# A trunk layer on one core: small products held behind the last large product traced ahead of them, with one or two more generator steps between some operands and their products

## The chip, the cores and the metric

The kernel runs on one core of one Trainium2 chip. The metric is device microseconds for one execution of the whole layer. Engines are named as in the profile: PE (TensorE matmul), DVE (VectorE), ACT (ScalarE), POOL (GpSimd), and SP, whose queue issues the DMAs.

## The reference

One layer of a conditioned decoder trunk, sequence 1024, width 1024. What matters here is the token mixer: one input projection feeds four branches of width 256, of which these are touched by the change:

```
def gla_chunked(q, k, v, log_a):            # 4 heads of 64
    def step(state, chunk):
        b = jnp.cumsum(lac, axis=2)
        q_dec = qc * jnp.exp(b)
        attn = jnp.where(causal, jnp.einsum('bhtd,bhsd->bhts', q_dec, kc * jnp.exp(-b)), 0.0)
        o = jnp.einsum('bhtd,bhde->bhte', q_dec, state) + jnp.einsum('bhts,bhse->bhte', attn, vc)
        k_dec = kc * jnp.exp(bL - b)
        state = jnp.exp(bL[:, :, 0, :])[..., None] * state + jnp.einsum('bhsd,bhse->bhde', k_dec, vc)
...
    a, g = jnp.split(p["conf"], 2, axis=-1)
    u = causal_dwconv(a * jax.nn.sigmoid(g), conf_dw_w) + conf_dw_b      # 31 taps
    u = jax.nn.silu(layer_norm(u, conf_ln_g, conf_ln_b))
...
    gates = jax.nn.sigmoid(p["gate"] + merge_gate_b).reshape(Bn, S, N_BRANCH, D_MODEL)
    merged = (gates[:, :, 0] * y_ml + ... + gates[:, :, 3] * y_sc)
    return merged @ w_o
```

An mLSTM branch of the same form as the gated linear attention (GLA) stands beside it. The layer ends with an output projection and a feed-forward part.

## The kernel before, in words

The weights are multiplied in a Strassen-like scheme: a pair of projections is made of seven large products (11, T2, 21, T1, T3, T4, 22), each of twelve 128x512 matmuls. The time runs through stages: the first norms and modulations; P, twelve such pairs (`pair`, called here P00 to P11); G, eight first halves of the gates (`gate_first`, numbered 0 to 7); then the rest of the gates with the merge (E), the output projection and the feed-forward part.

In P and G the branches' own small work runs between the large products. It is written as Python generators (`ml_all`, `gla_all`, `conf_mix` and what they call). After each large product `pull(rate, crate)` advances them by some steps, one step to the next `yield`. The scheduler then orders each engine by its own estimated timeline, so that a small product can move ahead of or behind the place where it was traced. POOL is kept in program order in P and G. The profile records every instruction at one line (159, a helper), so the source lines below are those of the program.

The pieces that the prediction speaks of:

- `tok_v` (line 891) turns the values of a branch from channel-major to token-major: eight transposes for each half of the channels, from a tile `p` that a DMA fills (`p<-dgv`). `tok_load` (line 904) issues both loads, but the second goes into the buffer that the first leaves free.
- `conf_mix` (line 805): 4 x 30 taps of the convolution on DVE (line 817) and a bias on ACT (820); sums over channels by a matrix of ones on PE (825), one group for each half of the sequence; DVE subtracts the mean (827); ACT squares (830, 831); sixteen one-column matmuls sum the squares (836).
- `gla_mix` (line 1116), eight chunks. For each chunk: scores, eight groups of small products `kx` by `qb` (1162), with operands from ACT exponentials and DVE multiplications in `prep` (1145, 1146); DVE masks the scores into `at` (1168); transposes of the decayed keys (1186), copied by ACT to `kw` (1188); the output from the state and from `at` (1191, 1194); then `kw` by `v`, which updates the state (1198).
- `gate_first` (line 634): first product (643), an ACT copy of its result (646), second product into the same accumulator (648), an ACT copy (651), a DMA to `dz` (652). The second product must wait for the first copy.

```
        prod(ps, wnext.pop(0), "11", True)
...
        A.copy(t[:, 0, :], ps)
        yield
        prod(ps, wnext.pop(0), "21", False)
...
        A.copy(t[:, 1, :], ps)
        nc.sync.dma_start(dz[4 * n + p], t)
```

- `lm[0]` holds the last large matmul that was traced; `prod` sets it.

Of the kernel before, what the change touches and what calls it, by code (L numbers as in the profile page):

```python
# [16 lines left out]
P = 128  # L17
# [129 lines left out]
def trunk_layer(ctx: ExitStack, tc: tile.TileContext, I, out, dump=None, stop=None):  # L147
# [14 lines left out]

    V, A, G, T = (InOrder(e, n) for e, n in ((nc.vector, "V"), (nc.scalar, "A"), (nc.gpsimd, "G"), (nc.tensor, "T")))
# [641 lines left out]
    def conf_mix():  # L805
# [16 lines left out]
        for h in range(2):  # L822
            ps = mps()
            for j in range(2):
                T.matmul(ps, ones, y[:, j, HH[h]], start=(j == 0), stop=(j == 1))
            for j in range(2):
                V.scalar_tensor_tensor(y[:, j, HH[h]], ps, -1.0 / MIX, y[:, j, HH[h]], ALU.mult, ALU.add)
            yield
# [5 lines left out]
        for a in range(NCH):  # L834
            for i, s_ in enumerate((s0, s1_)):
                T.matmul(ps[:, a:a + 1], s_[:, a * P:(a + 1) * P], one, start=(i == 0), stop=(i == 1))
# [3 lines left out]
        for h in range(2):  # L840
            ps = mps()
            rows_bc(r[:, 4 * h:4 * h + 4], 4, ps)
# [48 lines left out]
    def tok_v(v, j, vc):  # L891
        for h in range(2):
            ps = mps()
            for c in range(4):
                T.transpose(ps[:, c * P:(c + 1) * P], vc[:, (4 * h + c) * P:(4 * h + c + 1) * P], ident)
# [8 lines left out]
    def tok_load(nm):  # L904
# [5 lines left out]
        yield  # L910
        for j in range(2):
# [4 lines left out]
    def ml_all():  # L916
        vt = new_v("V")
        yield
# [13 lines left out]
    def ml_rows():  # L932
# [45 lines left out]
        for n, r in enumerate((a, w1, w0)):  # L978
            T.transpose(ps[:, 32 * n:32 * n + 32], r, ident[0:32, 0:32])
# [5 lines left out]
    def ml_mix(dnm, dwi, cols, v):  # L985
# [31 lines left out]
        for c in range(NCH):  # L1017
            e, q, kt, wi, qb = nxt_
            ps = mps()
            for j in range(2):  # L1020
                T.matmul(ps[:, j * MIX:(j + 1) * MIX], kt[:, j, :], qb[:, j].rearrange("p x t -> p (x t)"),
# [5 lines left out]
            for j in range(2):  # L1027
                T.transpose(pk[:, j * P:(j + 1) * P], kt[:, j, :], ident)
# [5 lines left out]
            for j in range(2):  # L1034
                w = 2 * (DH + 1)
                T.matmul(po[:, j * w:(j + 1) * w], qw[:, j, :], cn[:, j, :, :], start=True, stop=False)
                for x in range(2):
                    h = 2 * j + x
                    o = h * (DH + 1)
                    T.matmul(po[:, o:o + DH + 1], e[:, h, :], v[:, c, h, :], start=False, stop=(x == 1))  # L1040
# [7 lines left out]
            for j in range(2):  # L1048
                T.matmul(pc_[:, j * w:(j + 1) * w], kw[:, 2 * j:2 * j + 2, :], v[:, c, 2 * j:2 * j + 2, :],
# [17 lines left out]
    def head_norm(v, mul, dst):  # L1067
# [9 lines left out]
        for h in range(2):  # L1077
# [3 lines left out]
            for c in range(4):  # L1081
# [3 lines left out]
                for j in range(2):  # L1085
                    T.transpose(ps[j][:, c * P:(c + 1) * P], hf[:, j * P:(j + 1) * P], ident)
# [6 lines left out]
    def gla_decay():  # L1093
# [3 lines left out]
        for j in range(2):  # L1097
            t0, t1 = c4(), c4()
            for h in range(2):
                ps = mps()  # L1100
                T.matmul(ps, a2[64:96, j * P:(j + 1) * P], m2[64:96, HH[h]], start=True, stop=True)
# [14 lines left out]
    def gla_mix(v):  # L1116
# [37 lines left out]
        yield  # L1154
        for c in range(NCH):
# [3 lines left out]
            for j in range(2):  # L1159
                for i in range(NSB):  # L1160
                    m = (i + 1) * SB
                    T.matmul(ps4[0:m, j, :, i, :], kx[:, j, i, 0:m], qb[:, j, :, i * SB:m], start=True, stop=True)
# [15 lines left out]
            yield  # L1178
            if c + 1 < NCH:
                nxt_ = prep(c + 1, *raw1)  # L1180
            if c + 2 < NCH:
# [754 lines left out]
```

## Time and profile before

| | |
|---|---|
| median of 3 runs | 1636.38 us (1635.22 to 1641.09) |
| profiled execution | 1636.97 us, span 1635.2 us, so 1.8 us lie outside the span |
| PE busy | 1541.4 us, 94% of the span |
| DVE, ACT, POOL busy | 72%, 57%, 45% |
| mean granted TensorE clock | 0.97 |

Times in the views count from the start of the span. An operation's name is its output, an arrow, its inputs, by the program's names: `b` is a PSUM accumulator, `wh` and `wl` the two parts of a split weight, `cst` the identity, `cn` a branch's state.

### The profile page before, as it was taken

To read this page: it belongs to the slowest core of one execution; us is meant where nothing else is said; L and a number is where in the kernel's file an instruction comes from. 1 tells how busy PE (TensorE), PEld (TensorE's weight loads), DVE (VectorE), ACT (ScalarE), POOL (GpSimd) and SP (SyncE) were. 2 spreads that over 40 slices of the span, in tenths; PEclk is the share of its full clock that TensorE was granted. 3 is DMA by queue.
4 is the path that set the end of the run, shared out by engine and by line. 5 is a ranking of instruction groups with operands and counts; after the bars stand their busy time and mean duration, and the time that the engine had idled before them with its cause. 6 is when DMAs were issued, how large, how long until landed. Compare 5 with 4: busy or idle time off the path is not lost.

```text
span 1635.2 us, 21394 instructions
## 1 busy us (share of the span) xinstructions
PE 1541.4 (94%) x6885; PEld 1247.2 (76%) x6885; DVE 1179.4 (72%) x1955; ACT 928.8 (57%) x1718; POOL 732.5 (45%) x617
## 2 busy tenths in 40 slices
PE   7799799998998999999999999999999998999996
PEld 5677588876876777878788877778888887777885
DVE  7876886989555657766783769398888666555678
ACT  7465444344675453535454757566556655678973
POOL 1455365543343335747630224444445431866115
PEclk8799999999999999999999999999999999999997
DMA  9244325433357545454523564644444317455243
GB/s 363 69 148 130 100 88 148 130 110 106 104 191 242 159 142 164 127 184 129 173 78 97 193 213 149 208 152 162 140 155 142 99 65 256 158 167 178 66 129 122
DMA packets 133268, 242.70 MB, mean 148 GB/s; under 512 B 14052, under 2 KB 33092, under 8 KB 133156
## 3 DMA queue, kind: packets, MB, share of 16 engines
q1 hardware_dynamic: 132660, 241.10, 45.5%
q8 instruction: 54, 0.88, 0.2%
q14 instruction: 58, 0.48, 0.1%
q10 hardware_dynamic: 496, 0.23, 0.1%
HBM read 191.70 MB, written 49.58 MB: 148 GB/s over the span
## 4 chain that ended last, share of the span: by engine, by line
PE 70%; DVE 8%; DMA 8%; ACT 4%; issue 4%; POOL 2%; SPq 0%; DVEq 0%; POOLq 0%; ACTq 0%
PE b L159 70%; DVE c L159 2%; DVE wl L159 1%; DMA T<-dg 1%; DVE T L159 1%; DVE acc L159 1%; ACT b L159 1%; DMA s2d<-in_ada_b_dram 1%; ACT wh L159 1%; DMA wr<-in_wu_dram 1%; ACT B L159 1%; DVE B L159 1%; DMA c<-in_wt_dram 1%; DVE b L159 1%; DVE mg L159 1%
## 5 line engine op out<-in xcount | busy, mean ns | idle before, releaser
L159 PE MATMUL b<-B,wh 128*128 128x512 f32 (+1 forms) x1704 | 542.5, 401 | 30.5 <-DVE B L159 17.7
L159 PE MATMUL b<-T,wh 128*128 128x512 f32 x1512 | 482.9, 399 | 6.2 <-ACT wh L159 2.5
L159 PEld LDWEIGHTS b<-B,wh 128*128 128x128 f32 x1704 | 326.4, 195 | 103.7 <-DVE B L159 20.7
L159 PE MATMUL b<-B,wl 128*128 128x512 f32 (+1 forms) x840 | 335.2, 400 | 21.2 <-DVE wl L159 18.5
L159 PEld LDWEIGHTS b<-T,wh 128*128 128x128 f32 x1512 | 285.6, 190 | 73.2 <-ACT wh L159 3.4
L159 PE MATMUL b<-T,wl 128*128 128x512 f32 x752 | 298.0, 398 | 4.2 <-DVE wl L159 3.5
L159 PEld LDWEIGHTS b<-B,wl 128*128 128x128 f32 x840 | 162.9, 194 | 61.7 <-DVE wl L159 24.2
L159 PEld LDWEIGHTS b<-T,wl 128*128 128x128 f32 x752 | 142.7, 190 | 38.2 <-DVE wl L159 4.6
L159 ACT CAST wh<-wr 128x512 fp32r<-128x512 f32 x159 | 97.2, 616 | 112.0 <-PE b L159 81.6
L159 PE MATMUL b<-T,fh 128*128 128x512 f32 x368 | 116.2, 397 | 0.8 <-ACT fh L159 0.8
L159 DVE SCALAR_TENSOR_TENSOR b<-c,par,b 128x512 f32<-128x512 f32 x132 | 97.0, 751 | 25.9 <-ACT b L159 25.8
L159 DVE TENSOR_TENSOR c<-b,c 128x512 f32<-128x512 f32 x132 | 90.1, 685 | 19.5 <-PE b L159 15.2
L159 POOL TENSOR_TENSOR mg<-mg,c 128x512 f32<-128x512 f32 x48 | 63.0, 1332 | 75.6 <-DVE c L159 75.0
L159 ACT ACTIVATE c<-c,hpar 128x1024 f32<-128x1024 f32 (+1 forms) x34 | 37.5, 1104 | 102.2 <-DVE c L159 99.6
L159 DVE SCALAR_TENSOR_TENSOR b<-G,par,b 128x512 f32<-128x512 f32 x120 | 89.8, 748 | 1.3
L159 ACT ACTIVATE b<-c,par 128x512 f32<-128x512 f32 x88 | 57.4, 683 | 53.5 <-DVE c L159 53.1
L159 PEld LDWEIGHTS b<-T,fh 128*128 128x128 f32 x368 | 69.2, 188 | 17.9 <-ACT fh L159 1.2
L159 ACT CAST b<-wr 128x512 fp32r<-128x512 f32 x105 | 61.2, 586 | 35.3 <-DVE c L159 12.3
L159 PE MATMUL b<-B,wbh 128*128 128x512 f32 x256 | 80.4, 397 | 0.0
L159 DVE TENSOR_TENSOR wl<-wr,b 128x512 fp32r<-128x512 f32 x82 | 55.6, 681 | 25.0 <-ACT b L159 16.8
L159 PE MATMUL b<-T,fl 128*128 128x512 f32 x184 | 72.2, 395 | 0.0
L159 POOL TENSOR_TENSOR B<-B,B 128x512 f32<-128x512 f32 x29 | 43.3, 1492 | 59.7 <-DVE wl L159 56.6
(394 smaller groups left out, 2916.7 us busy)
## 6 DMA issues: line engine op xcount, KB each, us to landing
wr<-in_wu_dram SPq DMA_DIRECT2D x70, 256.0 KB, 2.7
B<-in_wg_dram SPq DMA_DIRECT2D x61, 256.0 KB, 3.5
fr<-in_wu_dram SPq DMA_DIRECT2D x50, 256.0 KB, 3.0
dg<-c SPq DMA_DIRECT2D x22, 512.0 KB, 2.9
T<-in_ada_a_dram SPq DMA_DIRECT2D x16, 512.0 KB, 9.5
wr<-in_wo_dram SPq DMA_DIRECT2D x32, 256.0 KB, 2.6
wr<-in_wp_dram SPq DMA_DIRECT2D x30, 256.0 KB, 2.8
wx<-in_wp_dram SPq DMA_DIRECT2D x24, 256.0 KB, 2.7
```

What stands on the lines that cost most here:

```text
L159: ins = f(*a, **k)
```

## The change

A class `Behind` wraps the tensor engine: each small product issued through `B` is placed after `lm[0]`, the last large matmul traced before it; the scheduler may not put it earlier on PE. It is used for the sums of `conf_mix`, the transposes of `tok_v`, the rows and chunks of the mLSTM, the head norms, and the decay and chunks of the GLA. Besides, `tok_load` gets two more `yield`s between the loads and the first transposes, `ml_all` two more, `gla_mix` one more ahead of its loop, and within a chunk `prep` of the next chunk moves ahead of a `yield`. The number of instructions stays the same on every engine; only their order changes, on PE from the place that ran at about 231 us to the one at 542 us.

```
+    class Behind:
+        def __getattr__(self, op):
+            def call(*a, **k):
+                with tc.issue_after(lm[0]):
+                    return getattr(T, op)(*a, **k)
+            return call
+
+    B = Behind()
...
             for j in range(2):
-                T.matmul(ps, ones, y[:, j, HH[h]], start=(j == 0), stop=(j == 1))
+                B.matmul(ps, ones, y[:, j, HH[h]], start=(j == 0), stop=(j == 1))
...
-                T.matmul(ps[:, a:a + 1], s_[:, a * P:(a + 1) * P], one, start=(i == 0), stop=(i == 1))
+                B.matmul(ps[:, a:a + 1], s_[:, a * P:(a + 1) * P], one, start=(i == 0), stop=(i == 1))
...
-            rows_bc(r[:, 4 * h:4 * h + 4], 4, ps)
+            with tc.issue_after(lm[0]):
+                rows_bc(r[:, 4 * h:4 * h + 4], 4, ps)
...
-                T.transpose(ps[:, c * P:(c + 1) * P], vc[:, (4 * h + c) * P:(4 * h + c + 1) * P], ident)
+                B.transpose(ps[:, c * P:(c + 1) * P], vc[:, (4 * h + c) * P:(4 * h + c + 1) * P], ident)
...
             nc.sync.dma_start(vcs[j], dp[nm][:, j, :])
         yield
         yield
+        yield
+        yield
         for j in range(2):
             tok_v(vt, j, vcs[j])
...
         vt = new_v("V")
+        yield
+        yield
         yield
...
-                    T.transpose(ps[j][:, c * P:(c + 1) * P], hf[:, j * P:(j + 1) * P], ident)
+                    B.transpose(ps[j][:, c * P:(c + 1) * P], hf[:, j * P:(j + 1) * P], ident)
...
         nxt_ = prep(0, *raw)
         yield
         yield
+        yield
         for c in range(NCH):
...
-                    T.matmul(ps4[0:m, j, :, i, :], kx[:, j, i, 0:m], qb[:, j, :, i * SB:m], start=True, stop=True)
+                    B.matmul(ps4[0:m, j, :, i, :], kx[:, j, i, 0:m], qb[:, j, :, i * SB:m], start=True, stop=True)
...
             G.tensor_tensor(kd, kd, k, ALU.mult)
-            yield
             if c + 1 < NCH:
                 nxt_ = prep(c + 1, *raw1)
+            yield
             if c + 2 < NCH:
                 raw1 = fetch(c + 2)
             yield
...
-                T.transpose(pk[:, j * P:(j + 1) * P], kd[:, j, :], ident)
+                B.transpose(pk[:, j * P:(j + 1) * P], kd[:, j, :], ident)
...
-                T.matmul(po[:, j * P:(j + 1) * P], qh[:, j, :], st[:, j, :, :], start=True, stop=False)
+                B.matmul(po[:, j * P:(j + 1) * P], qh[:, j, :], st[:, j, :, :], start=True, stop=False)
...
-                    T.matmul(po[:, h * DH:(h + 1) * DH], at[:, h, :], v[:, c, h, 0:DH], start=False, stop=(x == 1))
+                    B.matmul(po[:, h * DH:(h + 1) * DH], at[:, h, :], v[:, c, h, 0:DH], start=False, stop=(x == 1))
...
-                T.matmul(pst[:, j * P:(j + 1) * P], kw[:, j * P:(j + 1) * P], v[:, c, 2 * j:2 * j + 2, 0:DH],
+                B.matmul(pst[:, j * P:(j + 1) * P], kw[:, j * P:(j + 1) * P], v[:, c, 2 * j:2 * j + 2, 0:DH],
```

The same replacement of `T` by `B` stands in `ml_rows`, `ml_mix` and `gla_decay`.

**The GLA's values and the first sums of the convolution, on PE.** In both programs this is the stretch around P10's products T1 (`T_114`) and T3 (`T_123`); `cst,p` is a transpose of the values (first half `p_616`, second half `p_617`), `G,one` a sum of the convolution. Before:

```order
L159 MATMUL b_3220<-T_123_771,wh_3288 128x512 x2
L159 MATMUL b_3263<-cst_77,p_616_3212 128x128 x4
L159 MATMUL b_3269<-cst_77,p_616_3212 128x128 x4
L159 MATMUL b_3275<-T_114_712,wh_3256 128x512 x2
...
L159 MATMUL b_3220<-T_123_771,wl_3289 128x512
L159 MATMUL b_3302<-cst_77,p_617_3213 128x128 x4
L159 MATMUL b_3308<-cst_77,p_617_3213 128x128 x4
L159 MATMUL b_3324<-G_990,one_80 128x512 x2
L159 MATMUL b_3348<-G_990,one_80 128x512
```

and of the change:

```order
L159 MATMUL b_3220<-T_123_771,wl_3277 128x512
L159 MATMUL b_3290<-cst_77,p_616_3212 128x128 x4
L159 MATMUL b_3296<-cst_77,p_616_3212 128x128 x4
L159 MATMUL b_3302<-G_990,one_80 128x512 x2
L159 MATMUL b_3326<-cst_77,p_617_3213 128x128 x4
L159 MATMUL b_3332<-cst_77,p_617_3213 128x128 x4
L159 MATMUL b_3338<-G_990,one_80 128x512
```

The first eight transposes now stand behind T3 instead of at its head, and the second eight follow them with only two sums between, where T1 and most of T3 stood.

**The last sum, the squares and the scores of chunk 0, on PE.** This is between P11's first product (`B_22`) and its second (`T_104`); `s2c,c` with small shapes are the scores, `one,mi` the first column of squares. Before:

```order
L159 MATMUL b_3408<-B_22_118,wl_3377 128x512
L159 MATMUL b_3348<-G_990,one_80 128x512
L159 MATMUL b_3446<-s2c_3385,c_654_3389 32x2x32
...
L159 MATMUL b_3446<-s2c_3385,c_654_3389 128x2x32
L159 MATMUL b_3469<-one_80,mi_3402 128x1
L159 MATMUL b_3494<-T_104_660,wh_3421 128x512 x2
```

and of the change:

```order
L159 MATMUL b_3387<-B_22_118,wl_3367 128x512
L159 MATMUL b_3338<-G_990,one_80 128x512
L159 MATMUL b_3446<-one_80,mi_3381 128x1
L159 MATMUL b_3471<-T_104_660,wh_3400 128x512 x2
```

The scores have left this place (they now stand behind P11's fifth product), and the first column of squares follows the last sum at once.

On DVE the same stretch reads as follows; `b_2990<-G_990,par` is a tap of the convolution, `c_610` and `c_609` with `c_579`, `c_578` the short convolution's product (`post_sb`, 872), `c_609<-b` the end of P10's product 22. Before:

```order
L159 SCALAR_TENSOR_TENSOR b_2990<-G_990,par_76,b_2990 128x512
L159 TENSOR_TENSOR c_610_3165<-c_610_3165,c_579_2996 128x1024
L159 TENSOR_TENSOR wl_3422<-wr_3373,b_3423 128x512
L159 TENSOR_TENSOR c_609_3164<-b_3275,c_609_3164 128x512
L159 TENSOR_TENSOR s_674_3514<-p_639_3320 128x256
L159 TENSOR_TENSOR c_609_3164<-c_609_3164,c_578_2995 128x1024
```

and of the change:

```order
L159 TENSOR_TENSOR c_610_3165<-c_610_3165,c_579_2996 128x1024
L159 TENSOR_TENSOR c_609_3164<-b_3263,c_609_3164 128x512
L159 SCALAR_TENSOR_TENSOR b_2990<-G_990,par_76,b_2990 128x512
L159 TENSOR_TENSOR c_609_3164<-c_609_3164,c_578_2995 128x1024
L159 SCALAR_TENSOR_TENSOR b_2990<-G_990,par_76,b_2990 128x512 x2
L159 SCALAR_TENSOR_TENSOR G_990<-b_3338,G_990 128x512 x2
```

Before, all taps were ahead of the two wide products; now the last three taps stand behind the end of P10's product 22, and two of them behind a wide product.

**A chunk in the gates, on PE.** `cst,s` are the transposes of the decayed keys, `cn,s` and `V,s2b` or `V,s2a` the output, `V,s` the state's update; `B_24` to `B_31` are a gate's second product, `B_22` the first one of the next gate. Before:

```order
L159 MATMUL b_4396<-cst_77,s_846_4370 128x128 x2
L159 MATMUL b_4321<-B_24_120,wh_4279 128x512
...
L159 MATMUL b_4401<-cn_3314,s_845_4368 128x128
L159 MATMUL b_4415<-B_22_118,wh_4336 128x512 x2
...
L159 MATMUL b_4401<-V_3210,s2b_4360 128x64 x2
L159 MATMUL b_4401<-cn_3314,s_845_4368 128x128
L159 MATMUL b_4401<-V_3210,s2b_4360 128x64 x2
L159 MATMUL b_4415<-B_22_118,wh_4336 128x512 x2
L159 MATMUL b_4415<-B_22_118,wl_4337 128x512
L159 MATMUL b_4437<-V_3210,s_852_4399 128x128 x2
```

and of the change:

```order
L159 MATMUL b_4265<-B_30_126,wl_4237 128x512
L159 MATMUL b_4353<-cst_77,s_834_4306 128x128 x2
L159 MATMUL b_4358<-cn_3371,s_833_4304 128x128
L159 MATMUL b_4358<-V_3210,s2a_4296 128x64 x2
L159 MATMUL b_4358<-cn_3371,s_833_4304 128x128
L159 MATMUL b_4358<-V_3210,s2a_4296 128x64 x2
L159 MATMUL b_4365<-V_3210,s_843_4356 128x128 x2
L159 MATMUL b_4380<-B_22_118,wh_4280 128x512 x2
```

The small products of a chunk, which lay around and inside two large products, now stand in one batch behind the gate's second product; only the scores stand between a gate's two products, where before the state's update, the scores and the transposes did.

## Rows read from the trace of the kernel before

**Rows 1.** Windows: length, busy us (count) of PE, PEld, DVE, ACT, POOL; granted clock; DMA.

```profile
350.00:400.00 50.00, 47.75 (x210) 37.49 (x208) 48.34 (x68) 20.02 (x42) 20.30 (x14) 1.00 0.32 100
...
403.50:410.30 6.80, 5.77 (x20) 4.69 (x21) 3.98 (x13) 5.74 (x15) 0.00 (x0) 0.50 0.24 72
```

**Rows 2.** Timeline of PE: its waits above 0.3 us between 225 and 530 us.

```profile
295.95 0.70 PE L159 MATMUL b<-T,wh 128*128 128x512 f32 x2 [0.47 <-DVE cn L159]
...
338.62 0.41 PE L159 MATMUL b<-cst,s 128*128 128x128 f32 x2 [1.01 <-DVE s L159]
...
381.57 1.09 PE L159 MATMUL b<-cst,p 128*128 128x128 f32 x8 [2.25 <-DMA p<-dgv]
...
402.07 0.27 PE L159 MATMUL b<-s2c,c 128*32 128x64 f32 x2 [1.75 <-DVE c L159]
402.73 0.65 PE L159 MATMUL b<-s2c,c 128*64 128x64 f32 x4 [0.39 <-DVE c L159]
404.53 2.39 PE L159 MATMUL b<-s2c,c 128*128 128x64 f32 x10 [1.15 <-DVE c L159]
...
442.29 0.44 PE L159 MATMUL b<-cst,s 128*128 128x128 f32 x2 [0.80 <-POOL s L159]
...
452.26 0.27 PE L159 MATMUL b<-s2d,c 128*32 128x64 f32 x2 [2.20 <-DVE c L159]
...
524.80 1.19 PE L159 MATMUL b<-B,wh 128*128 128x512 f32 x2 [6.12 <-DVE c L159]
```

**Rows 3.** DMA issues between 370 and 392 us: KB each, us to landing.

```profile
p<-dgv SPq DMA_DIRECT2D x2, 512.0 KB, 4.0
```

**Rows 4.** Timeline of PE at the convolution's first three sums.

```profile
388.48 2.74 PE L159 MATMUL b<-G,one 128*128 128x512 f32 x6
```

**Rows 5.** Timeline of DVE at the end of the convolution.

```profile
394.66 0.75 DVE L159 SCALAR_TENSOR_TENSOR b<-G,par,b 128x512 f32<-128x512 f32 x1
395.31 1.73 DVE L159 TENSOR_TENSOR c<-c,c 128x1024 f32<-128x1024 f32 x1
...
397.56 0.68 DVE L159 TENSOR_TENSOR c<-b,c 128x512 f32<-128x512 f32 x1
...
398.97 2.30 DVE L159 TENSOR_TENSOR c<-c,c 128x1024 f32<-128x1024 f32 x1
...
402.87 1.28 DVE L159 SCALAR_TENSOR_TENSOR G<-b,G 128x512 f32<-128x512 f32 x2
```

**Rows 6.** Timeline of ACT: the convolution's bias, and its first squares.

```profile
397.19 0.68 ACT L159 ACTIVATE G<-b,par 128x512 f32<-128x512 f32 x1
...
403.58 1.06 ACT L159 ACTIVATE mi<-G 128x1024 f32<-128x1024 f32 x1 [1.77 <-DVE G L159]
```

**Rows 7.** Timeline of PE in one gate: scores, and the small products around its second product.

```profile
481.15 2.12 PE L159 MATMUL b<-s2c,c 128*32 128x64 f32 x16
483.10 0.39 PE L159 MATMUL b<-cst,s 128*128 128x128 f32 x2
...
486.08 0.38 PE L159 MATMUL b<-cn,s 128*128 128x128 f32 x2
...
488.39 0.55 PE L159 MATMUL b<-V,s2a 128*128 128x64 f32 x4
...
489.42 0.71 PE L159 MATMUL b<-B,wh 128*128 128x512 f32 x2
```

**Rows 8.** Timeline of ACT in the gates: copy of the keys, weight cast, result copy.

```profile
484.71 0.36 ACT L159 ACTIVATE s<-b 128x256 f32<-128x256 f32 x1
...
486.05 0.62 ACT L159 CAST wh<-wx 128x512 fp32r<-128x512 f32 x1 [0.67 <-PE b L159]
486.58 0.58 ACT L159 COPY c<-b 128x512 f32<-128x512 f32 x1
...
508.93 0.62 ACT L159 CAST wh<-B 128x512 fp32r<-128x512 f32 x1 [2.09 <-DMA B<-in_wg_dram]
509.46 0.58 ACT L159 COPY c<-b 128x512 f32<-128x512 f32 x1
```

More of the change, by code (lines that the diff above doesn't have):

```diff
@@ L978, in ml_rows @@
         for n, r in enumerate((a, w1, w0)):
-            T.transpose(ps[:, 32 * n:32 * n + 32], r, ident[0:32, 0:32])
+            B.transpose(ps[:, 32 * n:32 * n + 32], r, ident[0:32, 0:32])
         cols = new("cols", [P, 3, HEADS, NCH])
@@ L1020, in ml_mix @@
             for j in range(2):
-                T.matmul(ps[:, j * MIX:(j + 1) * MIX], kt[:, j, :], qb[:, j].rearrange("p x t -> p (x t)"),
+                B.matmul(ps[:, j * MIX:(j + 1) * MIX], kt[:, j, :], qb[:, j].rearrange("p x t -> p (x t)"),
                          start=True, stop=True)
@@ L1027, in ml_mix @@
             for j in range(2):
-                T.transpose(pk[:, j * P:(j + 1) * P], kt[:, j, :], ident)
+                B.transpose(pk[:, j * P:(j + 1) * P], kt[:, j, :], ident)
             kw = s1((P, HEADS, DH))
@@ L1035, in ml_mix @@
                 w = 2 * (DH + 1)
-                T.matmul(po[:, j * w:(j + 1) * w], qw[:, j, :], cn[:, j, :, :], start=True, stop=False)
+                B.matmul(po[:, j * w:(j + 1) * w], qw[:, j, :], cn[:, j, :, :], start=True, stop=False)
                 for x in range(2):
@@ L1039, in ml_mix @@
                     o = h * (DH + 1)
-                    T.matmul(po[:, o:o + DH + 1], e[:, h, :], v[:, c, h, :], start=False, stop=(x == 1))
+                    B.matmul(po[:, o:o + DH + 1], e[:, h, :], v[:, c, h, :], start=False, stop=(x == 1))
             if c + 1 < NCH:
@@ L1048, in ml_mix @@
             for j in range(2):
-                T.matmul(pc_[:, j * w:(j + 1) * w], kw[:, 2 * j:2 * j + 2, :], v[:, c, 2 * j:2 * j + 2, :],
+                B.matmul(pc_[:, j * w:(j + 1) * w], kw[:, 2 * j:2 * j + 2, :], v[:, c, 2 * j:2 * j + 2, :],
                          start=True, stop=True)
@@ L1100, in gla_decay @@
                 ps = mps()
-                T.matmul(ps, a2[64:96, j * P:(j + 1) * P], m2[64:96, HH[h]], start=True, stop=True)
+                B.matmul(ps, a2[64:96, j * P:(j + 1) * P], m2[64:96, HH[h]], start=True, stop=True)
                 A.activation(t1[:, HH[h]], ps, AF.Abs, bias=pc("glab", j))
```

## The prediction

> **What bounds the kernel now.** I read the busy time by stretch first, then the waits of PE, then the orders. PE bounds the kernel: of the 50 us from 350 to 400 it is busy 47.75 [rows 1]. In that same stretch DVE is busy 48.34, so DVE is nearly full exactly where the change moves most. PE's order differs only between about 231 and 542 us. So what the change can give is what PE idles there, and what it can cost is a new idle there; later stages keep their order on PE and move as one block.
>
> PE's waits in that stretch [rows 2] are eight behind small products, 0.47 + 1.01 + 2.25 + 1.75 + 0.39 + 1.15 + 0.80 + 2.20 = 10.0 us, and one of 6.12 us at 524.80, at the start of the merge, which is not a small product's. The reader should see that each of the eight is a small product put ahead of large ones whose operands were ready: the score groups of chunks 0 and 3 wait for DVE (`c`), eight transposes for a DMA.
>
> The waits of chunk 0 are followed by a stretch at clock 0.50, from 403.50 to 410.30, the 1.2 GHz level, with PE busy 5.77 us [rows 1]. Half of that, 2.9 us, is what the low clock cost there.
>
> **The change, part by part.** What it removes. In the new order all eight waiting products stand at least one large product later, and what they wait for is no later than before. I take the whole 10.0 us as gone; between 8 and 10.0, since an operand may be a little late still.
>
> What it adds, place by place, always as cover against chain:
>
> 1. Second half of the values. Its load can be issued only when the eighth transpose has freed the tile, and takes 4.0 us to land [rows 3]. Before, 6.9 us passed from the first eight at 381.57 [rows 2] to the sums at 388.48 [rows 4], which stand behind the second eight; less twice some 1.09 for the transposes themselves, that left 4.7 us of large products between, and the second half did not wait. Now only two sums lie between. Six such matmuls last 2.74 us [rows 4], so the four of two sums cover 1.8. Wait: 4.0 + 0.2 for the eighth's own end - 1.8 = 2.4 us. Behind the waiting transposes on PE stand the third sum and all of P10's T4. The lower bound is 0, if the load lands in less than 2 us; the upper is 3.4, if the first load too comes 1 us late, since SP now issues two weight loads ahead of it. I take 2.4. The Trainium skill, DMA: Bandwidth & Descriptors, section "Anatomy of one DMA — SWDGE (gpsimd) path", gives a DMA a fixed cost of about 2.0 us plus its bytes at 436 GB/s, though for a queue that GpSimd issues: by that 512 KB would take an estimated 3.2 us, the wait 1.6 and the whole sum 0.8 less. The measured 4.0 decides here.
>
> 2. The last of the convolution's sums. Its taps now stand on DVE behind the end of P10's product 22. From there DVE does one end operation (0.68), a tap (0.75), a wide product (1.73 or 2.30), two taps (1.5) [rows 5], and ACT the bias (0.68) [rows 6]: 5.3 to 5.9, or 4.9 where operations overlap by their 0.1. The cover is ten of the twelve matmuls of P11's first product. Twelve last 2.8 us (483.25, which is 0.15 behind the row at 483.10, to 486.08) [rows 7], so ten cover 2.4. Wait: 2.5 to 3.5, taken as 3.0. Before, all taps stood ahead of the wide products, and no wait is recorded at these sums. Queued behind: the squares and P11's second product.
>
> 3. The first column of squares now follows that sum directly. DVE subtracts the mean (half of 1.28, 0.64 [rows 5]), ACT squares (1.06 [rows 6]), and two handovers of some 0.1 to 0.15 each come with them: 2.0 us without any cover on PE. Before, the waiting scores of chunk 0 stood there and hid it. Bounds 1.7 and 2.5.
>
> 4. The gates. A gate's second product waits for the ACT copy of the first. Before, in the even cycle from 481 us on, the state's update, the scores and the transposes lay between; now the scores alone, 483.10 - 481.15 = 1.95 us [rows 7]. ACT needs a weight cast (0.53 to the next start) and the copy (0.58) [rows 8], 1.1 in all, so 0.85 us of slack is left: nothing, except at the first gate, where the convolution's last ACT operations of about 1 us stand ahead (0 to 1.0, taken as 0.5), and at the last one, where no scores are left between the products: 1.0 us.
>
> 5. The state's update now comes in the same batch as the transposes. Between them lie 0.3 us of transposes and first state product and 489.42 - 488.39 = 1.03 of the rest [rows 7], 1.3 in all. ACT does the cast (0.53 to the next start, from the end of the product at 486.05), the result copy (0.58) and the copy of the keys `kw` (0.36) [rows 8], less some 0.1 of overlap, 1.4 in all. That hardly fits: 0 to 0.3 in each of eight chunks, taken as 0.1, so 0.8.
>
> 6. At the end of the gates the ACT copy of the last result at 509.46 no longer stands behind the cast that had waited for a DMA and took 0.53 [rows 8]. The wait of 6.12 us at 524.80 hangs on that copy through a DMA to `dz`, a sigmoid and the merge, so it shrinks by 0.5. The head norm of the GLA comes nearer to its own operands and can make PE wait 2 to 3 us a little earlier; that is time taken out of the 6.12, not added, as long as it stays below it.
>
> Sum: -10.0 + 2.4 + 3.0 + 2.0 + 0.5 + 1.0 + 0.8 - 0.5 = -0.8 us. The low clock of 403.50 I leave in: the new waits of 3.0 and 2.0 lie as close together as the old 1.75, 0.39 and 1.15 that came ahead of it. Its bounds are -2.9 (it does not come) and +2.9 (one more stretch of the kind).
>
> The sum is made against the profiled execution, 1636.97 us (span 1635.2 and 1.8 around it), which is 0.6 above the median of the three runs, 1636.38. Against that median I forecast 1635.6.
>
> **The rivals.** *The waits go and nothing takes their place* (faster). For it: the order does take every waiting product behind a large one, and two steps more lie between operands and products. If DVE lets the taps through in time and the load lands in time, the sum is -10.0 - 0.5 and without a half-clock stretch another -2.9: 1623 to 1626. Against it: the three places above have no cover left on PE, and each chain is made of durations that stand in the rows. Chance 0.15. The Trainium skill, TensorE: Matmul & The Clock Gate, section "Part 1: The HAM clock gate (the "warmup" mystery)", lets the clock follow how busy PE has been; by it, fewer waits at 400 us would keep 2.4 GHz. The trace agrees so far as the 0.50 at 403.50 comes behind three waits.
>
> *ACT becomes the bound in the gates* (slower, the other side). The state's update waits for `kw`, which stands on ACT behind a weight cast and a result copy; both of these wait for PE's large product, so a late ACT can't work ahead. No slack is left in a chunk (point 5). If each cycle brings ACT one operation more between (a cast of 0.62, or a wait for a weight's DMA as the 2.09 at 508.93 [rows 8]), the wait is 0.5 to 2 us in each of eight chunks. From 1.1 us per chunk on, 9 us in all, the kernel is slower by over 0.5%; at 1.3 per chunk +10.4 less the 0.8 already counted and less the 0.8 of the sum give 1645. For it: the batch has hardly any slack. Against it: the cycle from 481 us has ACT idle 0.67 just ahead of that cast. Chance 0.12.
>
> *Only the clock decides*: waits as in my sum, but no low stretch (1632.7) or a second one (1638.5). Both within 0.5%. Chance 0.13 together.
>
> *The change does nothing*: the order shows that it moves what it says, so no chance is kept for it; a sum that ends at zero by balance is my own case.
>
> **How the numbers follow.** My case, with waits moved rather than removed, has 0.60 and gives 1631 to 1640 (each of the new waits at its bounds, not all at once). 0.5% is 8.2 us, about what a measurement of this kernel can tell from no change: below 1628.2 is faster, above 1644.6 slower. Faster: 0.15 of the first rival and 0.02 of the others' edge, 0.17. Slower: 0.10 of the second rival (the rest of it stays below the bound) and 0.02 from several waits at their upper ends, 0.12. Same: 0.71. The range for 8 in 10 takes my case and the clock whole, and part of both rivals: 1626 to 1643.
>
> **What would show it.** Right: in the profile of the changed kernel no wait of PE for DVE `c` at the scores of chunks 0 and 3, none at the first half of the values; a wait for `p<-dgv` of about 2.4 at the second half; one for ACT `G` of about 3 at the last sum; one for ACT `mi` of about 2 at the squares; no wait above 0.3 in the gates between; about 1 at the last gate; a wait at the head norm with a smaller one at the merge. Wrong: waits for ACT `s` (the keys) or `c` (the copy) above 0.5 in most gates, or none of the three in P10 and P11.

## The result, and the profile after

The changed kernel took 1647.97 us, median of five runs (1644.7 to 1652.35), against 1636.71 for the kernel before: a ratio of 1.0065, 95% interval 1.0043 to 1.0088. A second comparison gave medians of 1645.49 and 1635.05 (their quotient is 1.0064) and a ratio of 1.0056 (1.0038 to 1.0075). So it is slower, by 9 to 11 us; forecast was no change, 1635.6, and the time lies above the range.

The timeline of PE in the profile after, its waits above 1 us between 300 and 550 us, answers to [rows 2]:

```profile
388.24 1.09 PE L159 MATMUL b<-cst,p 128*128 128x128 f32 x8 [1.97 <-DMA p<-dgv]
...
404.45 2.08 PE L159 MATMUL b<-G,one 128*128 128x512 f32 x2 [4.38 <-ACT G L159]
408.40 0.58 PE L159 MATMUL b<-one,mi 128*128 128x1 f32 x2 [1.87 <-ACT mi L159]
...
446.49 0.73 PE L159 MATMUL b<-B,wh 128*128 128x512 f32 x2 [1.62 <-ACT c L159]
...
514.90 0.73 PE L159 MATMUL b<-B,wh 128*128 128x512 f32 x2 [1.23 <-ACT c L159]
...
519.80 1.75 PE L159 MATMUL b<-cst,s 128*128 128x128 f32 x10 [1.88 <-DVE s L159]
...
535.14 0.70 PE L159 MATMUL b<-B,wh 128*128 128x512 f32 x2 [4.42 <-DVE c L159]
...
545.56 0.50 PE L159 MATMUL b<-B,wl 128*128 128x512 f32 x1 [4.44 <-DVE wl L159]
```

None of the eight old waits is left, and each forecast place but one has its wait: the second half of the values, the last sum, the squares, the first and the last gate, the head norm. The missing one is the keys in the gates. One of the eight, at 295.95, was not a small product's: its row in [rows 2] is a large product, `T,wh`. New, and not forecast, is the size of the last line; before, the same product waited less (timeline of PE):

```profile
534.21 0.50 PE L159 MATMUL b<-B,wl 128*128 128x512 f32 x1 [2.69 <-DVE wl L159]
```

Why the last sum waits 4.38 us stands in DVE's timeline of the same profile:

```profile
392.35 0.74 DVE L159 SCALAR_TENSOR_TENSOR b<-G,par,b 128x512 f32<-128x512 f32 x1
394.85 1.18 DVE L159 TENSOR_TENSOR s<-p 128x256 f32<-128x256 f32 x1 [1.76 <-DMA p<-dgb]
...
396.55 0.74 DVE L159 SCALAR_TENSOR_TENSOR b<-G,par,b 128x512 f32<-128x512 f32 x1
...
398.20 1.22 DVE L159 TENSOR_TENSOR c<-c,c 128x1024 f32<-128x1024 f32 x1
399.34 0.68 DVE L159 TENSOR_TENSOR c<-b,c 128x512 f32<-128x512 f32 x1
399.94 0.74 DVE L159 SCALAR_TENSOR_TENSOR b<-G,par,b 128x512 f32<-128x512 f32 x1
400.59 1.63 DVE L159 TENSOR_TENSOR c<-c,c 128x1024 f32<-128x1024 f32 x1
402.14 1.53 DVE L159 SCALAR_TENSOR_TENSOR b<-G,par,b 128x512 f32<-128x512 f32 x2
...
406.56 1.29 DVE L159 SCALAR_TENSOR_TENSOR G<-b,G 128x512 f32<-128x512 f32 x2 [2.89 <-PE b L159]
```

From the end of product 22 (`c<-b`, 399.34) to the end of the last two taps the reader sees the five operations that point 2 listed, with the forecast lengths. But the row at 394.85 stands ahead of all of them: the GLA's first operation on its own loads, which idled DVE 1.76 us. The load that it waits for is `p<-dgb`. The timeline of SP shows its issue, and the DMA view of that issue the time to landing, before:

```profile
388.75 0.60 SPq L1123 DMA_DIRECT2D p<-dgb  x1
...
p<-dgb SPq DMA_DIRECT2D x1, 128.0 KB, 2.7
```

and after:

```profile
390.64 0.60 SPq L1136 DMA_DIRECT2D p<-dgb  x1
...
p<-dgb SPq DMA_DIRECT2D x1, 128.0 KB, 4.2
```

The issue is hardly later than before, if it is counted from the end of a wait near 205 us that both programs have (timeline of PE, first before, then after):

```profile
204.54 0.73 PE L159 MATMUL b<-T,wh 128*128 128x512 f32 x2 [1.81 <-ACT wh L159]
206.69 0.74 PE L159 MATMUL b<-T,wh 128*128 128x512 f32 x2 [1.79 <-ACT wh L159]
```

That is 184.2 us behind it before and 184.0 after. What differs is that the load took 1.5 us longer to land, and that DVE was ready for it 1.3 us sooner. Over the profiles used below, four of either kernel, the issue stands 183.6 to 184.9 us behind that wait before and 184.0 to 185.4 after, and the load landed in 2.4 to 2.7 us before and in 3.7 to 4.5 after; why it took longer is not shown.

ACT's part, and the first gate (timeline of ACT):

```profile
403.71 0.69 ACT L159 ACTIVATE G<-b,par 128x512 f32<-128x512 f32 x1 [3.13 <-DVE b L159]
407.29 1.06 ACT L159 ACTIVATE mi<-G 128x1024 f32<-128x1024 f32 x1 [2.89 <-DVE G L159]
...
444.91 1.06 ACT L159 ACTIVATE c<-c 128x1024 f32<-128x1024 f32 x1 [1.57 <-PE b L159]
445.87 0.57 ACT L159 COPY c<-b 128x512 f32<-128x512 f32 x1
```

At the first gate the copy at 445.87, for which PE's second product waits, stands behind an operation of the convolution of 1.06 us.

The clock, by windows of PE (length, busy us and count, granted clock, share and rate of DMA), before:

```profile
400.00:412.00 12.00, 8.72 (x37) 0.72 0.37 121
412.00:425.00 13.00, 13.00 (x90) 1.00 0.15 42
```

and after:

```profile
400.00:412.00 12.00, 5.75 (x13) 0.62 0.22 87
412.00:425.00 13.00, 13.00 (x61) 0.69 0.26 79
```

PE does less in the first window, and in the second, where it is busy without a gap, part of the work runs at the 1.2 GHz level.

To place the whole loss I cut each profile at two waits that every version has: the end of the wait for ACT `wh` near 205 us and the end of the wait for DVE `wl` near 540 us. Between them the time is split into idle of PE, loss to the low clock (half the busy time at clock 0.50), and the rest, work at full clock, from windows of 0.5 us. Four profiles of either kernel are at hand, one of before with other code only behind this stretch:

```
                     time   idle   low clock   work
before              329.7   18.8     7.1      303.7
before, 2nd         331.6   18.0    10.2      303.4
before, 3rd         331.1   18.9     8.2      303.9
before, fill @ 970  332.9   17.2    12.2      303.6
after               338.9   22.1    12.0      304.8
after, 2nd          338.1   23.3    10.4      304.3
after, 3rd          339.6   23.3    12.0      304.2
after, 4th          339.5   23.1    12.1      304.2
```

Means: 331.3 before, 339.0 after. Of the 7.7 us, idle is 4.7 and never overlaps; the low clock is 2.2, and overlaps; work is 0.7. The remaining 1.5 to 3.5 us lie outside, where the order is the same and single profiles of one kernel differ as much (from the `wl` wait to the wait near 970 us: 436.1, 438.4, 432.8 before, 439.9, 437.6, 437.6, 438.0 after).

### The profile page after: what moved, and what is told of

Its sections match the earlier page's. It is cut to its first block, busy times and chain, and to the rows that moved or that the text cites. A ratio compares the mean times of both kernels' runs of the same rounds, so it can differ in the third digit from the quotient of the medians.

```text
span 1650.6 us, 21394 instructions
## 1 busy us (share of the span) xinstructions
PE 1551.3 (94%) x6885; PEld 1248.7 (76%) x6885; DVE 1181.6 (72%) x1955; ACT 928.5 (56%) x1718; POOL 725.9 (44%) x617
## 4 chain that ended last, share of the span: by engine, by line
PE 62%; issue 8%; DVE 7%; DMA 7%; ACT 3%; POOL 2%; SPq 0%; DVEq 0%; POOLq 0%; ACTq 0%
PE b L159 62%; DVE c L159 2%; DVE wl L159 1%; DVE T L159 1%; DVE acc L159 1%; DMA s2d<-in_ada_b_dram 1%; DMA s2a<-in_ada_b_dram 1%; ACT b L159 1%; POOL mg L159 1%; DMA wr<-in_wu_dram 1%; DVE b L159 1%; DMA c<-dg 1%; ACT wh L159 0%; ACT c L159 0%; DMA dz<-c 0%
## 5 line engine op out<-in xcount | busy, mean ns | idle before, releaser
L159 PE MATMUL b<-B,wh 128*128 128x512 f32 (+1 forms) x1704 | 543.5, 401 | 30.3 <-DVE B L159 18.5
L159 PE MATMUL b<-B,wl 128*128 128x512 f32 (+1 forms) x840 | 335.6, 401 | 22.7 <-DVE wl L159 19.2
```

The lines of the kernel that those rows point to most:

```text
L159: ins = f(*a, **k)
```

## The experiments

Two theories stood at the start. A: the cost is the last sum and the second half of the values, which the loads' added pulls bring late. B: it is the pinning (`B` for `T`), which leaves chains of ACT and DVE in the gates without cover. The kernels are parts of the change; "pins" is every `B`, "loads" the two pulls in `tok_load`, "ml" the two in `ml_all`, "GLA" the edits in `gla_mix`.

**Pins alone**, no pull added (in `tok_load` and `ml_all`, and `gla_mix` with its old `yield`s):

```
         yield
-        yield
-        yield
         for j in range(2):
             tok_v(vt, j, vcs[j])
...
```

> The added pulls are taken out again; every small product is still held behind its large product. Two theories for the changed kernel's +11 us. A: it is lost between P10 and the first gates, where the second half of the values, the last sum and the squares lost their cover, and each new wait brings a stretch of low clock. B: it is lost by the pinning itself, in the gates, where a chunk's products wait for ACT. In this order T1 and most of T3 stand between the two halves of the values again. A: about the time of before, 1632 to 1640, no wait for p<-dgv at the second half, and no more half-clock time from 385 to 455 us than the 6.8 us of before. B: 1644 or more.

Measured: 1.0005 (0.9990 to 1.0021). So the pins alone cost nothing that shows, against theory B. Theory A's second sign did not come: from 385 to 455 us the mean granted clock was 0.89, which is some 16 us at half clock where A allowed 6.8.

**All pulls, no pins:**

```
-                with tc.issue_after(lm[0]):
-                    return getattr(T, op)(*a, **k)
+                return getattr(T, op)(*a, **k)
...
```

> The added pulls stay, but no product is held behind a large one. PE's order up to P11's third product is then that of the changed kernel; it differs only in the gates. A: the waits for p<-dgv (2.0), ACT G (4.4) and ACT mi (1.9) stay, with 10 us or more of half clock behind them; 1643 to 1649. B: they may stay, but the kernel is back below 1640, since the gates are free.

Measured: 1.0017 (1.0001 to 1.0034), so a small cost is left, and the time of 1639.79 us is the one that B named. Its last sum waits 5.86 us for ACT `G`, more than in the first profile of the changed kernel, and yet the loss is a quarter of it: that wait is not the whole cause, against theory A.

**The change without the loads' pulls** (against the changed kernel):

```
         yield
         yield
-        yield
-        yield
         for j in range(2):
             tok_v(vt, j, vcs[j])
```

> Of the changed kernel only the two pulls in tok_load are taken out. T1 and T3 stand between the two halves of the values again; the pinning and all other pulls stay. A: the wait at the second half goes, one of about 2 comes back at the first half, the GLA's loads start earlier and the wait for ACT G falls from 4.4 to 1 to 3; 1636 to 1643. B: 1646 or more.

Measured: 1.0037 (1.0023 to 1.0051). No wait at the last sum; instead 4.45 us at the first half of the values, 2.71 at the squares and 3.83 at the first gate. The time, 1642.38 us, lies in A's range, but not by A's waits. The interval overlaps that of the changed kernel, so a gain by this alone is not settled.

**The change without the GLA's edits:**

```
         yield
         yield
-        yield
         for c in range(NCH):
...
-            if c + 1 < NCH:
-                nxt_ = prep(c + 1, *raw1)
             yield
+            if c + 1 < NCH:
+                nxt_ = prep(c + 1, *raw1)
```

> Of the changed kernel only gla_mix's edits to its yields are taken out (one less ahead of the loop, prep behind the first yield again); pinning and the pulls of tok_load and ml_all stay. The waits at the values, the last sum and the squares are upstream of this and should stay (2.0, 4.4, 1.9). If the loss lies there: 1641 to 1648. If it lies in the gates' new cycle, where scores alone stand between a gate's two products: 1638 or less, and no wait at the gates' second products.

Measured: 1.0028 (1.0018 to 1.0038); the last sum waits 5.81, the first gate 0.68. The time, 1639.79 us, lies between the two forecasts: some 5 us of the loss go with these edits, though the three waits ahead stay.

**The loads' pulls alone, on the kernel before:**

```
+        yield
+        yield
         for j in range(2):
             tok_v(vt, j, vcs[j])
```

> The kernel before with one edit: the two more pulls in tok_load. Nothing is pinned. PE's order then has both halves of the values behind T3, and sum and squares side by side, as in the changed kernel. If the loss lies there (A): waits of about 2.0, 4 to 6 and 1.9 for p<-dgv, ACT G and ACT mi, half clock behind them, and 2 to 8 us above before. If the pinning is needed for it: within 2 us of before.

Measured: 0.9992 (0.9979 to 1.0006). The second half of the values waits 2.04 and the squares 1.87, as in the changed kernel, but the last sum only 0.49 (timeline of PE of this run):

```profile
401.16 1.12 PE L159 MATMUL b<-G,one 128*128 128x512 f32 x2 [0.49 <-ACT G L159]
```

Its DVE meets the same GLA operation without idling, and no tap is left behind the end of product 22 (`c<-b`, 400.30) where the changed kernel has three (timeline of DVE):

```profile
394.51 1.12 DVE L159 TENSOR_TENSOR s<-p 128x256 f32<-128x256 f32 x1
...
399.64 0.74 DVE L159 SCALAR_TENSOR_TENSOR b<-G,par,b 128x512 f32<-128x512 f32 x1
400.30 0.68 DVE L159 TENSOR_TENSOR c<-b,c 128x512 f32<-128x512 f32 x1
401.01 1.23 DVE L159 TENSOR_TENSOR c<-c,c 128x1024 f32<-128x1024 f32 x1
402.32 1.29 DVE L159 SCALAR_TENSOR_TENSOR G<-b,G 128x512 f32<-128x512 f32 x2
```

**The GLA's edits alone, on the kernel before:**

```
         yield
         yield
+        yield
         for c in range(NCH):
...
-            yield
             if c + 1 < NCH:
                 nxt_ = prep(c + 1, *raw1)
+            yield
```

> The kernel before with gla_mix's edits to its yields alone (one more ahead of the loop, prep ahead of the first yield); nothing is pinned and no other pull added. Taken off and added one by one under pinning, these edits were worth about 5 us. If that is their own: 1639 to 1642. If they cost only together with the pinning, as the pulls of tok_load do: within 2 us of before.

Measured: 0.9990 (0.9976 to 1.0005). Theory A and theory B both fall as single causes: neither the pins, nor the loads' pulls, nor the GLA's edits cost anything that shows alone. (The `ml` pulls were not run alone.)

**Pins in the two mixers only, with the GLA's edits** (convolution and `tok_v` left on `T`, no pull in `tok_load` and `ml_all`), against the changed kernel:

```
-                B.matmul(ps, ones, y[:, j, HH[h]], start=(j == 0), stop=(j == 1))
+                T.matmul(ps, ones, y[:, j, HH[h]], start=(j == 0), stop=(j == 1))
...
-                B.transpose(ps[:, c * P:(c + 1) * P], vc[:, (4 * h + c) * P:(4 * h + c + 1) * P], ident)
+                T.transpose(ps[:, c * P:(c + 1) * P], vc[:, (4 * h + c) * P:(4 * h + c + 1) * P], ident)
...
```

> Pinning in the rows and chunks of mLSTM and GLA, the head norms and the decay, and gla_mix's edits; the convolution's sums and the transposes of the values are free, and tok_load and ml_all have their old yields. PE's order then has T1 and T3 between the halves of the values. If the loss comes with the late values: within 2 us of before. If it comes with pinning and gla_mix's edits: 1640 to 1643, with a wait of 1 to 4 us at the first gate's second product.

Measured: 1.0031 (1.0016 to 1.0046). The first gate waits 4.39 for the ACT copy, the squares 2.10, the merge 3.80. So with pins the GLA's edits cost 4 to 6 us (1.0031 here against 1.0005 for the pins alone; 1.0028 without these edits against 1.0056 to 1.0065 with them), without pins nothing.

**Pins and the `ml` pulls alone**, since both kernels that leave a part out still hold these (`tok_load` and `gla_mix` with their old `yield`s); the pulls, against the kernel before:

```
         vt = new_v("V")
+        yield
+        yield
         yield
```

> The pinning of the small products, and of the added pulls only the two in ml_all. The pinning alone measured 1.0005, with the loads' pulls and these 1.0028, with the GLA's pulls and these 1.0037. Theory 'the pulls cost where they bring the values and the gates late': these two act near 231 us only, so 1.000 to 1.002, with no wait above 4 us at the last sum. Rival 'the cost that the two kernels share is that of these pulls': 1.0025 or more.

Measured: 1.0009 (0.9996 to 1.0022), as the first theory said.

**The change without the `ml` pulls:**

```
         vt = new_v("V")
-        yield
-        yield
         yield
```

> The changed kernel without the two pulls in ml_all: pinning, the loads' pulls and the GLA's. First theory: as the changed kernel, 1.005 to 1.0065, with the wait of 4 to 6 us at the last sum and 8.5 us or more of loss at half clock up to the merge. Rival: these pulls carry part of the cost, then 1.004 or less.

Measured: 1.0037 (1.0022 to 1.0052), with a wait of only 1.15 us at the last sum. That fits the rival's number, but the interval overlaps that of the changed kernel, and its stretch from 205 to 540 us takes 339.3 us, no less than the 339.0: not settled. What it does show is that the long wait at the last sum needs both the loads' and the `ml` pulls: it was 4.4 to 6.3 us where both are in, 0 to 1.2 where one is missing. Other waits stand in its place: PE waits 0.92 us for DVE `cn` at 297.07 and 2.11 for DVE `s` at 340.69, where the changed kernel waits 0 to 0.74 near 297 us and not near 340. So the loss in the stretch does not hang on the one wait at the last sum.

The same stretch in the parts, by the cut of above:

```
pins  pulls            ratio    time   idle   low clock
no    loads            0.9992   331.0  17.4     8.3
no    GLA              0.9990   327.3  17.2     5.1
no    all              1.0017   333.7  19.2    10.4
yes   none             1.0005   332.8  18.1    10.2
yes   ml               1.0009   332.1  16.8    11.1
yes   loads, ml        1.0028   334.6  21.2     8.8
yes   GLA, ml          1.0037   336.7  20.7    11.9
part  GLA              1.0031   338.1  22.3    11.6
yes   loads, GLA       1.0037   339.3  21.2    13.3
yes   all              1.0065   338.9  22.1    12.0
```

Idle is the column to read: 16.8 to 19.2 us, as before, without pins or without the loads' and the GLA's pulls; 20.7 to 23.3 with pins and either of them. Each row is one profile. By the times the cost is in good part an interplay of the two: 1.0005 for the pins and 1.0017 for all pulls would add up to 1.0022, and together they measured 1.0056 and 1.0065.

**The changed kernel with the last sum's wait filled:** 18 matmuls of zeros ahead of it, on whose result nothing rests.

```
         prod(pa, w11, "11", True)
+        if not following:
+            z = mps()
+            for _ in range(18):
+                with tc.issue_after(lm[0]):
+                    T.matmul(z, wz[:, 0:P], wz, start=True, stop=True)
```

> The changed kernel with 18 matmuls of zeros (bf16, 128x512, about 0.21 us each, 3.8 us) put on PE between P11's first product and the last sum, where PE waits 4.4 us for ACT G. They change no operand. A, with the clock as about 7 of the 11 us: the wait shrinks to below 1 us, the half clock from 402 to 424 us goes for the most part, and the time falls to 1639 to 1644. If the clock does not follow PE's idle, or its low stretches cost nothing: 1646 to 1650, as without the filling.

Measured: 1.0019 (1.0004 to 1.0034). The time, 1639.46 us, is in A's range, but a wait of 1.22 us is left and the half clock is not gone for the most part: 0.86 from 400 to 412 us and 0.74 from 412 to 425. The same kernel a second time:

> The changed kernel with 18 matmuls of zeros, which change no operand, ahead of the last sum; it measured 1.0019 once, but its profile showed 327 us up to the merge, no less than the changed kernel's 327 to 329. Theory 'the low clock at the last sum makes the difference': again below 1.003, and up to the merge 325 us or less. Rival 'the gain was the execution's': 1.0035 or more.

Measured: 1.0019 again (1.0007 to 1.0032), and 325.1 us up to the merge, at the bound of what the theory wanted (the first time 327.4). PE's timeline there:

```profile
399.06 4.06 PE L159 MATMUL b<-one 128*128 128x512 bf16 x17
402.95 1.02 PE L159 MATMUL b<-G,one 128*128 128x512 f32 x2
405.85 0.38 PE L159 MATMUL b<-one,mi 128*128 128x1 f32 x2 [1.87 <-ACT mi L159]
```

and the same windows as above, here and in the first profile of the filled kernel:

```profile
400.00:412.00 12.00, 10.13 (x59) 1.00 0.11 44
412.00:425.00 13.00, 13.00 (x64) 0.87 0.37 113
...
400.00:412.00 12.00, 8.90 (x36) 0.86 0.15 60
412.00:425.00 13.00, 13.00 (x61) 0.74 0.35 104
```

The sum itself took 2.08 us in the changed kernel, behind its wait, and 1.02 here. From the last matmul of P11's first product to the first one behind the squares, the changed kernel took 17.2, 18.6, 19.2 and 19.0 us in its four profiles, the filled ones 16.6 and 13.0: 2 and 5.5 us below the mean of the four, 18.5. So the low clock behind this wait is a part of the loss, though the wait itself only changed its name. How large a part is open: the stretch from 205 to 540 us takes 336.5 and 336.0 us, only some 3 less than the changed kernel's 339.0, while the ratios differ by 6 to 7.5 us.

**A second fill,** eight such matmuls ahead of the second half of the values as well:

```
+                for _ in range(fill):
+                    with tc.issue_after(sums_[-1]):
+                        T.matmul(ps, wz[:, 0:P], wz, start=True, stop=True)
...
```

> The changed kernel with zeros' matmuls in two of its waits: 18 ahead of the last sum, as before, and 8 (1.7 us) behind the first two sums, where PE waits 2.0 us for the second half of the values. A: the half clock after the second half of the values (3.4 us) goes too, so 1 to 2 us below the kernel with one filling. If the short wait is not what brings that stretch: the same as with one filling.

Measured: 1.0039 (1.0025 to 1.0053), no better than one fill. That wait falls to 0.32 us, but the work grows (309.7 us, with one fill 308.0 and 308.4, without 304.4) and the loss to the low clock is 11.5, with one fill 10.2.

**The kernel before with a fill** of 18 at its wait near 970 us:

```
+                if t0:
+                    for _ in range(18):
+                        T.matmul(pcs, wz[:, 0:P], wz, start=True, stop=True)
```

> The kernel before with 18 matmuls of zeros (3.8 us) at one of its own waits, far from the change: ahead of the column sums at 970 us, where PE waits 3.6 us for DVE and runs 6.8 us at half clock afterwards. The zeros go into the accumulator that the sums then start anew. If the idle of PE is what brings the low clock: the wait becomes filled, the half clock from 970 to 977 us goes, the stretch from 966 to 1011 us is 2.5 to 3.5 us shorter, and the time 1 to 4 us below before. If not: half clock as before, and the time the same or up to 0.5 us longer.

Measured: 0.9997 (0.9981 to 1.0012), a miss for the gain. The wait and the half clock behind it are gone from the profile, where the zeros start at 974.62 (window: length, then busy us of PE, PEld, DVE, ACT and POOL, clock, DMA),

```profile
974.00:990.00 16.00, 15.89 (x79) 11.58 (x78) 10.64 (x22) 11.42 (x22) 2.88 (x3) 1.00 0.80 290
```

and that place is 2.5 us shorter, but the whole is not.

**The same kernels again.** The changed kernel, timed and profiled once more:

> The changed kernel once more, unaltered, beside the others on one chip, for a second profile and a time with more runs. If the first time was typical: 1644 to 1650, with about 24 us of half clock from 385 to 455 us and the same waits to 0.3 us. If part of its +11 us was chance of those executions: 1639 to 1643, with fewer half-clock stretches.

Measured: 1.0056 (above); its waits are 1.96, 5.54, 1.87, 1.62, 1.22, 1.87, 3.38 and 5.12. The time is as the first, but three waits moved by more than 0.3 us, and from 385 to 455 us the mean granted clock was 0.88 where the first profile had 0.83. Then two more profiles of each:

> The kernel before, unchanged, profiled once more. In the first profile the stretch from the end of the wait for `wh` near 205 us to the merge wait near 525 us took 320.3 us, of which 4.6 us are the loss at half clock and 16.1 us idle of PE. Theory 'the half clock belongs to the change': again 4 to 6 us of loss there. Theory 'it belongs to the execution': the loss wanders between 4 and 10 us, as it read 10.2 us in a kernel with the same code in this stretch.

> The kernel before a third time. Theory 'the half clock belongs to the change': 4 to 6 us of loss and some 320 us in the stretch; theory 'it belongs to the execution': anywhere from 4 to 10 us and 320 to 325 us. After the merge wait, the stretch to the wait near 970 us: 445 us in the first profile; if the order there costs nothing of its own this wanders by as much as it differs from the changed kernel's 450 us.

> The changed kernel, unchanged, profiled once more. In its two profiles the stretch from the wait for `wh` near 205 us to the merge wait took 328.4 and 327.2 us, 10.2 and 8.9 us of it loss at half clock and 17.6 and 18.2 us idle. Theory 'the half clock belongs to the change': a loss of 8.5 us or more again, and the low stretch 402 to 424 us again. Theory 'it belongs to the execution': a loss anywhere from 4 to 10 us, and the time of the stretch down to 322 us with it.

> The changed kernel a fourth time. Theory 'the half clock belongs to the change': 8.5 us or more of loss and 327 to 329 us in the stretch up to the merge wait; theory 'it belongs to the execution': 4 to 10 us and 322 to 329 us. From the merge wait to the wait near 983 us: 450 and 448.5 us in the two profiles so far; as low as 445 us in one of the two would take the difference behind the merge away from the change.

Measured: 1641.07 and 1632.59 us before, 1645.6 and 1642.44 after, single runs. Up to the merge wait: 322.0 and 321.8 before, 328.7 and 328.8 after; loss at low clock 8.5 and 6.2 against 10.4 and 10.6. With the other profiles of the same code the time is 320.3 to 324.5 before and 327.2 to 328.8 after, and does not overlap: it belongs to the change. The loss at low clock is 4.6 to 10.2 before and 8.9 to 10.6 after, and does overlap: it wanders by some 5 us between profiles of the kernel before.

## Why the prediction was wrong, point by point

The step that failed is the sum of the new waits: −0.8 us was forecast, and the measured waits give +4.4. Of the 5.2 us between them 2.6 are point 2, the wait at the last sum, 1.5 the end of the gates (point 6) and 1.1 the first gate (point 4); the other points cancel. The rest of the 9 to 11 us stood in no term at all or in the clock's: 2.2 of low clock, 0.7 of work, 1.5 to 3.5 outside the stretch. Four profiles after, three before where nothing else is said.

- **What is removed.** All eight waits went, as forecast, though a large product near 297 us waits 0.45 to 0.74 us in three of the four profiles, and the one at 295.95 was a large product's too. Their sum before was 10.0, 8.3 and 9.6, mean 9.3: 0.7 less to win than one profile said.
- **Point 1, second half of the values:** 1.97, 1.96, 2.04, 2.04 against 2.4. Right. (The load landed in 3.7 us. By the 3.2 that the Trainium skill, DMA: Bandwidth & Descriptors, section "Anatomy of one DMA — SWDGE (gpsimd) path", led me to estimate, the wait was to be 1.6; the measured wait lies between that and 2.4.)
- **Point 2, last sum: the step that failed most.** 4.38, 5.54, 6.29, 6.01, mean 5.6, against 3.0 with an upper bound of 3.5. The chain behind the end of product 22 was sized rightly. The forecast let it start 2.4 us ahead of the end of P11's first product; it started 1.7, 2.8, 3.6 and 3.3 us later than that, which is the excess of the wait over 3.0 to within 0.3. That this end would itself stand on DVE behind a GLA operation that waits for a DMA was not priced: DVE idled 1.76, 1.12, 2.23 and 2.05 us there, and 0.31 to 0.91 more for ACT behind it. I asked what is late next on PE, and not on DVE. No kernel takes DVE's idle alone away, so its share of the wait is read from the timeline and not tested.
- **Point 3, squares:** 1.87 in all four, against 2.0. Right. (In the rows above the handovers take 0.03 to 0.05 us each, not 0.1 to 0.15.)
- **Point 4, gates:** last gate 1.22 to 1.25 against 1.0; first gate 1.62 in all four against 0.5, above its bound of 1.0: the operation of ACT ahead of the copy itself waits for PE (1.57), so its whole 1.06 and the copy count.
- **Point 5, keys:** nothing against 0.8. ACT has the slack; the rival "ACT becomes the bound in the gates" did not come.
- **Point 6, end of the gates:** head norm and merge together went from 6.1 to 5.4, a little more than the 0.5 forecast. But the product behind the merge waits 4.4 to 5.1 where it waited 2.7 to 3.7, so the three together rose from 9.2 to 10.2. That the time taken out of the merge comes back one product later was the second missing step; why it does is not shown.
- **The sum.** With the measured waits, and 0.4 us of small new ones near 297 us: 2.0 + 5.6 + 1.9 + 1.6 + 1.2 + 0.4 = 12.7 for 9.3, and 1.0 at the end: +4.4 where −0.8 stood. The cut of the stretch gives +4.7 of idle.
- **The clock.** Left in with bounds of ±2.9; 2.2 more by the means, inside the bounds but all on one side, and the filled kernels point to the longer wait at the last sum for part of it. The forecast read the low stretch of the kernel before as coming behind three waits; its third, the 1.15 us that end at 404.53, lies within the stretch, which starts at 403.50. The Trainium skill, TensorE: Matmul & The Clock Gate, section "Part 1: The HAM clock gate (the "warmup" mystery)", has the clock follow how busy PE has been. The trace agrees where a fill kept 1.00 between 400 and 412 us; in the other profile of the same filled kernel it read 0.86.
- **The rivals.** "The waits go and nothing takes their place" fell with the first profile. "Only the clock decides" is part of it, but no more.

Range: my case had each new wait at its bound "not all at once"; in fact the misses that weigh were in one direction. That much of the cost needs both pins and pulls is what the part kernels show. A likely way, argued and not tested: added pulls make operands late, and pins forbid a late small product, and what stands behind it, to change places. Open remains the split of the low clock between change and execution, the 1.5 to 3.5 us outside the stretch, and what the `ml` pulls add. No kernel of these beats the one before: 0.9990 and 0.9992 lie within what can be told.

## What to carry to other kernels

Pinning small products cost nothing that shows (1.0005), delaying all their operands little (1.0017), and together they cost 9 to 11 us: change one of them at a time, and measure both orders before stacking. When a product is put behind a large one, follow the queues of the engines that feed it to the first operation that waits for a DMA; here the start of the chain was late by 1.7 to 3.6 us, with such a wait of 1.1 to 2.2 us ahead of it. A wait that shrinks counts as gain only after the next wait of the same chain has been read.

## What was not expected of the hardware

The clock fell with no wait right ahead of it: in the changed kernel PE went from 413.70 to 417.30 without idle through 30 records of one-column products (timeline of PE),

```profile
413.70 0.28 PE L159 MATMUL b<-one,c 128*128 128x1 f32 x2
...
417.30 1.20 PE L159 MATMUL b<-B,wh 128*128 128x512 f32 x2
418.30 0.63 PE L159 MATMUL b<-B,wl 128*128 128x512 f32 x1
```

and the large products behind it ran at 0.63 us each, where they take 0.39 at the 2.4 GHz level. The windows of the same profile, and, last, one of the kernel before (length, busy us and count of PE, clock, DMA), are

```profile
413.30:416.50 3.20, 3.20 (x29) 1.00 0.29 82
416.70:423.30 6.60, 6.60 (x18) 0.50 0.23 74
...
411.89:415.30 3.41, 3.41 (x33) 1.00 0.00 0
```

The last line is the same run of one-column products in the kernel before, and there the clock stayed at 1.00 up to 425 us. So these products do not bring the fall by themselves; what else does is not shown. And the low clock is no fixed property of a program: the code of before lost between 7.1 and 12.2 us to it in one and the same stretch.
